# Attention logits by joined products, alternating heads, and a router constant made on VectorE, in a two-layer decoder trunk

## The chip, the cores and the metric

The kernel runs on one core of a Trainium2 chip. A core has five engines with queues of their own: TensorE (PE in the rows; its weight loads are PEld) multiplies matrices into PSUM, VectorE (DVE) and ScalarE (ACT) work element by element, GpSimd (POOL) is a slower third one for that, and SyncE (SP) here issues the loads from HBM. The metric is the time of one execution on the device in microseconds, the median of several.

## What is computed

Two layers over 256 tokens of width 1024. Each has a mixer and then 16 experts of which every token takes two. The parts that the change touches:

```
# layer 0, attention: 8 heads of width 64, blocks of 128 queries
z = einsum('bhqd,bhkd->bhqk', q[:, :, start:end], k[:, :, :end])
strict = s_pos < t_pos
log_keep = where(strict, log_sigmoid(-z), 0.0)
later = cumsum(log_keep, axis=3, reverse=True) - log_keep
a = where(strict, exp(log_sigmoid(z) + later), 0.0)
out = einsum('bhqk,bhkd->bhqd', a, v[:, :, :end])
# layer 1, gated linear attention: 4 heads of key width 64
scores = where(causal, einsum('nbhid,nbhjd->nbhij', q_in, k_in), 0.0)
# both layers, the experts' router
h = rmsnorm(x, norm_ffn[l]) * (1.0 + sc2) + sh2
scores = softmax(h @ router_w)
```

Since h is a scaled x plus a shift sh2 that is the same for all tokens, the router's logits are a product of x with scaled weights plus a constant, sh2 @ router_w, that holds for every token.

## The kernel before

The program is written out by hand: each engine runs its instructions in the order in which the code issues them, and waits on semaphores where an operand is not there or a buffer not free. Weights come through a ring of 16 buffers of 1 MB (`unit`, L67 and L69, and `weight`, L1224), loaded by SyncE in the order of their use as soon as a buffer is free. Jobs of the modulation vectors (`ada`, L188: products of 32 columns each) are put between other products by `fill`.

Layer 0 runs projections and convolution taps (`conv`: some taps on VectorE at L541, some on ScalarE at L555 and GpSimd at L556), then from about 106 to 151 us the attention in `even_mixer`. Its four steps cc take one pair of heads each; the keys and queries of the two heads lie on partitions 0 to 63 and 64 to 127 of `kT` and `qT`. `logits` (L602 to L606) makes z for both heads of a pair in two PSUM banks, one bank per head, 384 columns: 256 queries against the first 128 keys, 128 against the second 128, and a mask of large negative numbers that is added as a bf16 product of the identity with `maskb` to each diagonal block. `minus` (ScalarE L612, VectorE L614), `softplus` (ScalarE L618, L619) and `softplus2` (VectorE L622) turn z into what `sums` (TensorE L629 to L632) adds up; `weights` (VectorE L636, L637, ScalarE L638) gives the attention weights, `attend` (L649, L650) their products with the values, for head 0 on output partitions 0 to 63 and for head 1 on 64 to 127, and `attended` (ScalarE L654, VectorE L655) cuts the result in two parts. `logits` of pairs 0 and 1 stand ahead of the loop, those of 2 and 3 in its first two rounds.

After it come the group norm of the convolution (`group_norm`, L660 on) and the output products `po` (L451), whose weights ScalarE (L55) and VectorE or GpSimd (L56) cut into two parts first. Ahead of the second half of them, `Norm.weights` makes the gain gc (L365), the router's scaled weights rwg (L372, VectorE) and the router's constant rc (L375): 8 single-precision products on TensorE, whose left operand is one modulation column spread over 128 columns. Layer 1 does the same ahead of its own second half. ScalarE copies rc out of PSUM (L378); the route uses it after the logits.

A single-precision product appears in the trace as two passes (two weight loads and two MATMUL rows). In layer 1 `attention` is a generator of which every `yield` is followed by one step of a projection; its gated scores gs (L911) are two groups of four products, for heads with q = 0 (partitions 0 to 63) and q = 1 (64 to 127), each followed by the copies of the causal part (VectorE, L915). The products kv (L926) work on partitions 0 to 63 and 64 to 127 too, with outputs on either half of the partitions and in two banks.

Of the kernel before, what the change touches and what calls it, by code (L numbers as in the profile page):

```python
# [7 lines left out]
F32 = mybir.dt.float32  # L8
# [4 lines left out]
OP = mybir.AluOpType  # L13
AX = mybir.AxisListType
# [3 lines left out]
E = 16  # L18
# [11 lines left out]
def trunk(ctx: ExitStack, tc: tile.TileContext, x, c, ada_w, ada_b, norm_mix, norm_ffn,  # L30
# [5 lines left out]
    V, S, G, PE, SP = nc.vector, nc.scalar, nc.gpsimd, nc.tensor, nc.sync  # L36
# [3 lines left out]
    live = ctx.enter_context(tc.tile_pool(name="live", bufs=1))  # L40
# [3 lines left out]
    def bank(name):  # L44
        return psum.tile([128, 512], F32, tag="ps", name=name)
# [51 lines left out]
    ones = const.tile([128, 128], F32, name="ones")  # L97
# [29 lines left out]
    b = bank("vcol")  # L127
# [46 lines left out]
    arow = {}  # L174
# [78 lines left out]
    class Norm:  # L253
# [113 lines left out]
        def weights(self):  # L367

            l = self.l
            self.gain()  # L370
            self.w = live.tile([128, 8, E], F32, tag="rwg", name=f"rwg{l}")
            V.tensor_tensor(self.w, rw, self.g[:, :, None].to_broadcast([128, 8, E]), op=OP.mult)  # L372
            b = bank(f"rc{l}")
            for k in range(8):
                PE.matmul(b[:, 0:E], lhsT=mod[l][:, 3, k:k + 1].to_broadcast([128, 128]), rhs=rw[:, k, :],  # L375
                          start=k == 0, stop=k == 7)
            self.c = live.tile([128, E], F32, tag="rc", name=f"rc{l}")
            S.activation(self.c, b[:, 0:E], AF.Copy)  # L378

# [115 lines left out]
    def even_mixer(pool, n01, late):  # L495
# [100 lines left out]
        def logits(cc):  # L596

            z = zl[cc] = zz.tile([128, 2, 512], F32, tag="zz", name=f"z{cc}")
            for h2 in range(2):
                r = slice(64 * h2, 64 * h2 + 64)  # L600
                zh = z[:, h2]
                PE.matmul(zh[:, 0:128], lhsT=identb, rhs=maskb, start=True, stop=False)  # L602
                PE.matmul(zh[:, 0:128], lhsT=kT[r, cc, 0:128], rhs=qT[r, cc, 0:128], start=False, stop=False)
                PE.matmul(zh[:, 128:256], lhsT=kT[r, cc, 0:128], rhs=qT[r, cc, 128:256], start=False, stop=False)
                PE.matmul(zh[:, 256:384], lhsT=identb, rhs=maskb, start=False, stop=False)
                PE.matmul(zh[:, 256:384], lhsT=kT[r, cc, 128:256], rhs=qT[r, cc, 128:256], start=False, stop=True)  # L606


        def minus(cc):
# [33 lines left out]
        def attend(cc):  # L643
            ob = zl[cc] = bank(f"att{cc}")
            a = zs[cc]
            for h2 in range(2):
                hc = slice((2 * cc + h2) * 64, (2 * cc + h2) * 64 + 64)
                r = slice(64 * h2, 64 * h2 + 64)
                PE.matmul(ob[r, 0:256], lhsT=vn[:, 0, hc], rhs=a[:, h2, 0:256], start=True, stop=False)  # L649
                PE.matmul(ob[r, 128:256], lhsT=vn[:, 1, hc], rhs=a[:, h2, 256:384], start=False, stop=True)  # L650

        def attended(cc):
            hi, lo = (c[:, 4 + cc, :] for c in cats)
# [130 lines left out]
    def odd_mixer(pool, nrm, n11, late, project):  # L784
# [62 lines left out]
        def attention():  # L847
# [54 lines left out]
            V.tensor_copy(kdn, halves(b))  # L902
            yield

            for q in range(2):
                b = bank(f"gs{q}").rearrange("p (c i) -> p c i", c=4)
                o = slice(64 * q, 64 * q + 64)
                for t in range(2):
                    ts_ = slice(t * 128, t * 128 + 128)
                    for cc in range(2):  # L910
                        PE.matmul(b[:, 2 * t + cc, :], lhsT=kT[o, cc, ts_], rhs=qT[o, cc, ts_], start=True, stop=True)  # L911
                yield
                for t in range(2):
                    for cc in range(2):
                        V.copy_predicated(sc[:, t, 2 * cc + q], trii, b[:, 2 * t + cc, :])  # L915
            yield
            yield

            yield
# [732 lines left out]
```

## Time and profile before

| | us |
|---|---|
| median of 3 runs (795.85 to 861.59) | 797.86 |
| the profiled execution | 801.36 |
| its span, first to last instruction | 799.6 |
| TensorE busy | 736.6 (92%) |
| VectorE, ScalarE, GpSimd busy | 314.4, 235.1, 118.9 |
| loads: 280.59 MB read, mean | 352 GB/s |
| a convolution tap on VectorE (L541, 56 of them), mean | 0.736 |

Times in the rows count from the start of the span. A timeline row has the start, the length of the row from its first start to its last end, engine, line, operation, output and inputs, shapes and count; in brackets the idle time of the engine before it and what ended it. Layer 0's mixer lasts until about 200 us, its experts until about 415, layer 1's mixer until about 560, its experts until the end.

### The profile page before, as it was taken

Reading aid. Unit: us, or ns where it says so; the run is one execution under the profiler, and the core shown is the slowest. Engines: PE = TensorE matmul, PEld = TensorE weight load, DVE = VectorE, ACT = ScalarE, POOL = GpSimd, SP = SyncE. Lnnn points to the kernel's source line nnn. Section 1 sums busy time; section 2 is a strip of 40 time slices with the busy share of each in tenths; the row PEclk is TensorE's granted clock in tenths of the full one; section 3 lists DMA queues with packets and bytes.
Section 4 is the critical chain, followed back from the end, with each engine's and each line's share of the span. In section 5 each row is a group of like instructions: output and inputs, shape, how many; then the busy total and the mean of one; then the engine's idle time right before and its main releaser. Section 6 shows DMA issues by size and latency. Waiting matters only on the chain. (4 is left out here: it accounts for less than half of the span.)

```text
span 799.6 us, 10666 instructions
## 1 busy us (share of the span) xinstructions
PE 736.6 (92%) x4177; PEld 404.3 (51%) x4177; DVE 314.4 (39%) x563; ACT 235.1 (29%) x441; POOL 118.9 (15%) x168
## 2 busy tenths in 40 slices
PE   7898798998999999999697999999699999999985
PEld 4498555586434344353233677578434334434323
DVE  4459968575213112130115655453513123213114
ACT  3357647463102001110113543551402001001012
POOL 2347646222000000000014500010200000000000
PEclk9999989999999999999989999999899999999988
DMA  9999739954999999999999997495799999999991
GB/s 358 385 376 419 267 120 394 372 224 192 351 412 409 409 409 409 410 408 409 407 401 389 401 413 247 182 390 204 292 362 411 410 409 409 410 410 409 408 381 58
DMA packets 74718, 282.52 MB, mean 353 GB/s; under 512 B 5194, under 2 KB 6438, under 8 KB 69530
## 3 DMA queue, kind: packets, MB, share of 16 engines
q1 hardware_dynamic: 73122, 278.68, 89.0%
q0 software_dynamic: 1344, 2.64, 0.9%
q8 instruction: 37, 0.61, 0.3%
q10 hardware_dynamic: 184, 0.34, 0.1%
q14 instruction: 31, 0.25, 0.1%
HBM read 280.59 MB, written 1.05 MB: 352 GB/s over the span
## 5 line engine op out<-in xcount | busy, mean ns | idle before, releaser
L1240 PE MATMUL g<-w,xg 128*64 128x512 f32 x512 | 115.9, 601 | 1.9 <-DMA w<-in_moe_w_gate_dram 1.8
L1273 PE MATMUL dn<-w,at 128*64 128x512 f32 x448 | 105.6, 623 | 11.5 <-PEq L1372 5.7
L1240 PE MATMUL u<-w,xg 128*64 128x512 f32 x496 | 110.6, 594 | 1.9 <-DMA w<-in_moe_w_up_dram 1.9
L1273 PEld LDWEIGHTS dn<-w,at 128*64 128x64 f32 x448 | 32.3, 143 | 77.0 <-issue 59.9
L1252 DVE TENSOR_TENSOR act<-sg,u 128x512 f32<-128x512 f32 (+1 forms) x18 | 11.1, 628 | 152.6 <-PE u L1240 152.6
L1240 PEld LDWEIGHTS u<-w,xg 128*64 128x64 f32 x496 | 34.7, 137 | 71.6 <-issue 64.7
L1240 PEld LDWEIGHTS g<-w,xg 128*64 128x64 f32 x512 | 35.3, 138 | 69.4 <-issue 62.9
L421 PE MATMUL pj<-hT,g 128*128 128x256 f32 x480 | 62.5, 288 | 7.0 <-DVE g L56 4.6
L56 DVE TENSOR_TENSOR g<-wi,g 128x512 fp32r<-128x512 f32 x72 | 58.2, 816 | 25.6 <-ACT g L55 24.5
L421 PEld LDWEIGHTS pj<-hT,g 128*128 128x128 f32 x480 | 59.2, 193 | 10.7 <-DVE g L56 6.7
L416 PE MATMUL pj<-g,hT 128*128 128x512 f32 x192 | 51.2, 414 | 7.5 <-DVE g L56 3.6
L55 ACT ACTIVATE g<-wi 128x512 fp32r<-128x512 f32 x72 | 44.4, 626 | 39.7 <-PE pj L421 20.9
L451 PE MATMUL po<-cat,g 128*128 128x256 f32 x372 | 51.1, 290 | 2.5 <-ACT gsr L994 1.7
L188 PE MATMUL ada<-ad,cond 128*32 128x512 f32 x384 | 50.6, 632 | 0.0
L451 PEld LDWEIGHTS po<-cat,g 128*128 128x128 f32 x372 | 46.8, 196 | 6.7 <-ACT gsr L994 2.6
L416 PEld LDWEIGHTS pj<-g,hT 128*128 128x128 f32 x192 | 35.6, 194 | 22.3 <-DVE g L56 6.7
L556 POOL TENSOR_TENSOR yc<-yc,cv 128x256 f32<-128x256 f32 x45 | 38.7, 860 | 24.3 <-ACT cv L555 21.6
L541 DVE SCALAR_TENSOR_TENSOR yc<-yp,epar,yc 128x256 f32<-128x256 f32 x56 | 41.2, 736 | 1.0
L1305 ACT ACTIVATE ys<-y 128x512 fp32r<-128x512 f32 x28 | 16.9, 625 | 70.4 <-DVE y L1295 50.2
L1263 DVE COPY at<-at 128x512 f32<-128x512 f32 x14 | 9.7, 692 | 68.0 <-PE at L1262 68.0
L1299 ACT ACTIVATE y<-dn,cw 128x512 f32<-128x512 f32 x7 | 4.8, 687 | 107.4 <-PE dn L1273 107.4
L1248 ACT ACTIVATE sg<-g 128x512 f32<-128x512 f32 x14 | 8.4, 597 | 89.4 <-PE g L1240 86.3
(385 smaller groups left out, 886.4 us busy)
## 6 DMA issues: line engine op xcount, KB each, us to landing
w<-in_moe_w_gate_dram SPq DMA_DIRECT2D x64, 1024.0 KB, 16.1
w<-in_moe_w_up_dram SPq DMA_DIRECT2D x62, 1024.0 KB, 18.4
w<-in_moe_w_down_dram SPq DMA_DIRECT2D x61, 1024.0 KB, 18.2
ad<-in_ada_w_dram SPq DMA_DIRECT2D x48, 1024.0 KB, 8.9
wi<-in_w_in_even_dram SPq DMA_DIRECT2D x20, 512.0 KB, 13.0
wi<-in_w_in_odd_dram SPq DMA_DIRECT2D x14, 512.0 KB, 12.6
wo<-in_w_out_even_dram SPq DMA_DIRECT2D x4, 1024.0 KB
wo<-in_w_out_odd_dram SPq DMA_DIRECT2D x4, 1024.0 KB, 16.6
```

The lines of the kernel that those rows point to most:

```text
L55: S.activation(g[0], w, AF.Copy)
L56: (eng or V).tensor_tensor(g[1], w, g[0].bitcast(F32), op=OP.subtract)
L188: PE.matmul(acc[32 * j:32 * j + 32, :], lhsT=cond[:, k, :], rhs=w[:, k - (i if n == 2 else 2 * i), c0:c0 + 512], start=i == 0, stop=i == 4 ...
L416: PE.matmul(bs[t], lhsT=self.h[j][:, k, t * 128:(t + 1) * 128], rhs=g[i], start=k == 0 and p == 0, stop=k == 7 and p == 2)
L421: PE.matmul(bs[c // 2][:, (c % 2) * T:(c % 2 + 1) * T], lhsT=g[i][:, c * 128:(c + 1) * 128], rhs=self.h[j][:, k, :], start=k == 0 and c % ...
L451: PE.matmul(self.acc[kd // 2][:, (kd % 2) * T:(kd % 2 + 1) * T], lhsT=block(g[wi], kd % 4), rhs=cats[ci][:, k, :], start=start and kd % 2 ...
L541: V.scalar_tensor_tensor(yc[:, k], yp[:, k, j:j + T], epar[:, k, j:j + 1], yc[:, k], op0=OP.mult, op1=OP.add)
L556: G.tensor_tensor(y, y, p, op=OP.add)
L1240: PE.matmul(b[64 * e:64 * e + 64, :], lhsT=xg[:, k, o + 64 * e:o + 64 * e + 64], rhs=we[:, e, k % 2 * 512:k % 2 * 512 + 512], start=k == 0 ...
L1252: V.tensor_tensor(a[:, n], sg[:, n], ub[:, n], op=OP.mult)
L1273: PE.matmul(bs[h][64 * e:64 * e + 64, :], lhsT=at[k][:, 64 * e:64 * e + 64], rhs=r[:, e], start=k == 0, stop=k == 3)
L1305: S.activation(ys[:, 0, n], y[h], AF.Copy)
```

## The change

Four edits. In `logits` the two blocks of queries against the first 128 keys become one product of 256 columns, products of the two heads alternate, and one mask product per head over both diagonal blocks comes last. In `attend` the loops are exchanged. In layer 1 the products of the gated scores alternate between q = 0 and q = 1 in one group, and the copies follow in the two steps behind it. In `Norm.weights` the constant is summed over the 8 column blocks by a multiplication and a sum on VectorE (by_k, of_p), and one product with a matrix of ones adds over the partitions.

```diff
@@ Norm.weights
+            by_k = live.tile([128, E, 8], F32, tag="arow", name=f"rk{l}")
+            V.tensor_tensor(by_k.rearrange("p e k -> p k e"), rw, mod[l][:, 3, :, None].to_broadcast([128, 8, E]), op=OP.mult)
+            of_p = live.tile([128, E], F32, tag="ap", name=f"rp{l}")
+            V.tensor_reduce(of_p, by_k, axis=AX.X, op=OP.add)
             b = bank(f"rc{l}")
-            for k in range(8):
-                PE.matmul(b[:, 0:E], lhsT=mod[l][:, 3, k:k + 1].to_broadcast([128, 128]), rhs=rw[:, k, :],
-                          start=k == 0, stop=k == 7)
+            PE.matmul(b[:, 0:E], lhsT=ones, rhs=of_p, start=True, stop=True)
@@ logits
+            heads = [slice(64 * h2, 64 * h2 + 64) for h2 in range(2)]
+            for h2, r in enumerate(heads):
+                PE.matmul(z[:, h2, 0:256], lhsT=kT[r, cc, 0:128], rhs=qT[r, cc, :], start=True, stop=False)
+            for h2, r in enumerate(heads):
+                PE.matmul(z[:, h2, 256:384], lhsT=kT[r, cc, 128:256], rhs=qT[r, cc, 128:256], start=False, stop=False)
             for h2 in range(2):
-                r = slice(64 * h2, 64 * h2 + 64)
-                zh = z[:, h2]
-                PE.matmul(zh[:, 0:128], lhsT=identb, rhs=maskb, start=True, stop=False)
-                PE.matmul(zh[:, 0:128], lhsT=kT[r, cc, 0:128], rhs=qT[r, cc, 0:128], start=False, stop=False)
-                PE.matmul(zh[:, 128:256], lhsT=kT[r, cc, 0:128], rhs=qT[r, cc, 128:256], start=False, stop=False)
-                PE.matmul(zh[:, 256:384], lhsT=identb, rhs=maskb, start=False, stop=False)
-                PE.matmul(zh[:, 256:384], lhsT=kT[r, cc, 128:256], rhs=qT[r, cc, 128:256], start=False, stop=True)
+                PE.matmul(z[:, h2].rearrange("p (a t) -> p a t", a=2)[:, :, 0:128], lhsT=identb,
+                          rhs=maskb[:, None, :].to_broadcast([128, 2, 128]), start=False, stop=True)
@@ attend
-            for h2 in range(2):
-                hc = slice((2 * cc + h2) * 64, (2 * cc + h2) * 64 + 64)
-                r = slice(64 * h2, 64 * h2 + 64)
-                PE.matmul(ob[r, 0:256], lhsT=vn[:, 0, hc], rhs=a[:, h2, 0:256], start=True, stop=False)
-                PE.matmul(ob[r, 128:256], lhsT=vn[:, 1, hc], rhs=a[:, h2, 256:384], start=False, stop=True)
+            for t in range(2):
+                for h2 in range(2):
+                    hc = slice((2 * cc + h2) * 64, (2 * cc + h2) * 64 + 64)
+                    r = slice(64 * h2, 64 * h2 + 64)
+                    PE.matmul(ob[r, 128 * t:256], lhsT=vn[:, t, hc], rhs=a[:, h2, 256 * t:256 + 128 * t],
+                              start=t == 0, stop=t == 1)
@@ attention (layer 1)
-            for q in range(2):
-                b = bank(f"gs{q}").rearrange("p (c i) -> p c i", c=4)
-                o = slice(64 * q, 64 * q + 64)
-                for t in range(2):
-                    ts_ = slice(t * 128, t * 128 + 128)
-                    for cc in range(2):
+            bs = [bank(f"gs{q}").rearrange("p (c i) -> p c i", c=4) for q in range(2)]
+            for t in range(2):
+                ts_ = slice(t * 128, t * 128 + 128)
+                for cc in range(2):
+                    for q, b in enumerate(bs):
+                        o = slice(64 * q, 64 * q + 64)
                         PE.matmul(b[:, 2 * t + cc, :], lhsT=kT[o, cc, ts_], rhs=qT[o, cc, ts_], start=True, stop=True)
-                yield
+            yield
+            for q, b in enumerate(bs):
                 for t in range(2):
                     for cc in range(2):
                         V.copy_predicated(sc[:, t, 2 * cc + q], trii, b[:, 2 * t + cc, :])
-            yield
+                yield
             yield
```

In TensorE's queue the logits of pair 0 stood as follows: z_1078 is their PSUM tile, and both heads carry the same names, first head 0 from a mask to the next but one, then head 1.

```order
L602 LDWEIGHTS identb
L602 MATMUL z_1078<-maskb,identb 128x128
L603 MATMUL z_1078<-qT,kT 128x128
L604 MATMUL z_1078<-qT,kT 128x128
L605 LDWEIGHTS identb
L605 MATMUL z_1078<-maskb,identb 128x128
L606 MATMUL z_1078<-qT,kT 128x128
L602 LDWEIGHTS identb
L602 MATMUL z_1078<-maskb,identb 128x128
L603 MATMUL z_1078<-qT,kT 128x128
```

Now, at the same place, a row with x2 holds the product of head 0 and then that of head 1:

```order
L604 MATMUL z_1078<-qT,kT 128x256 x2
L606 MATMUL z_1078<-qT,kT 128x128 x2
L608 LDWEIGHTS identb
L608 MATMUL z_1078<-maskb,identb 128x2x128
L608 LDWEIGHTS identb
L608 MATMUL z_1078<-maskb,identb 128x2x128
```

Ten products have become six, and the masks have moved behind the products of both heads.

On VectorE, in layer 0 at the end of the weight cuts (g are cut weights, gc the gain, rwg the router's scaled weights, xT the residual), there stood:

```order
L56 TENSOR_TENSOR g_1617<-wo_1551,g_1617 128x512
L56 TENSOR_TENSOR g_1623<-wo_1549,g_1623 128x512
L365 SCALAR_TENSOR_TENSOR gc_1633<-mod_148,vcol 128x8
L372 TENSOR_TENSOR rwg_1635<-rw,gc_1633 128x128
L479 SCALAR_TENSOR_TENSOR xT<-po_1452,mod_148,xT 128x256 x2
```

and now there stands (rk is by_k, rp is of_p):

```order
L56 TENSOR_TENSOR g_1601<-wo_1535,g_1601 128x512
L56 TENSOR_TENSOR g_1607<-wo_1533,g_1607 128x512
L365 SCALAR_TENSOR_TENSOR gc_1617<-mod_148,vcol 128x8
L372 TENSOR_TENSOR rwg_1619<-rw,gc_1617 128x128
L374 TENSOR_TENSOR rk_1621<-rw,mod_148 128x8x16
L376 TENSOR_REDUCE rp_1623<-rk_1621 128x16
L481 SCALAR_TENSOR_TENSOR xT<-po_1436,mod_148,xT 128x256 x2
```

Two instructions have come in behind the last cuts.

On TensorE the same place reads, before (acol is a modulation column, po the output products, cat the mixer's result in two parts):

```order
L451 MATMUL po_1455<-cat_1077,g_1534 128x256
L451 MATMUL po_1455<-cat_1076,g_1534 128x256
L197 MATMUL acol_1626<-ident,arow_1446 128x128 x4
L375 MATMUL rc_1637<-rw,mod_148 128x16 x8
L451 MATMUL po_1452<-cat_1076,g_1553 128x256
L451 MATMUL po_1452<-cat_1077,g_1553 128x256
```

and now:

```order
L453 MATMUL po_1439<-cat_1077,g_1518 128x256
L453 MATMUL po_1439<-cat_1076,g_1518 128x256
L197 MATMUL acol_1610<-ident,arow_1430 128x128 x4
L378 MATMUL rc_1625<-rp_1623,ones 128x16
L453 MATMUL po_1436<-cat_1076,g_1537 128x256
L453 MATMUL po_1436<-cat_1077,g_1537 128x256
```

The one product that is left reads rp of VectorE, and stands where the eight stood, ahead of the second half of the output products. Layer 1 has the same order on both engines.

## Rows read from the trace of the kernel before

**Rows 1.** The page, rate of the transfers, 40 equal slices of the span.

```profile
GB/s 358 385 376 419 267 120 394 372 224 192 351 412 409 409 409 409 410 408 409 407 401 389 401 413 247 182 390 204 292 362 411 410 409 409 410 410 409 408 381 58
```

**Rows 2.** Busy time by window: PE, PEld, DVE, ACT, POOL, clock, DMA, GB/s.

```profile
185.00:188.00 3.00, 3.00 (x29) 3.00 (x27) 0.88 (x2) 0.05 (x1) 0.00 (x0) 1.00 0.02 8
...
218.00:221.00 3.00, 3.00 (x18) 1.00 (x16) 0.88 (x2) 0.00 (x0) 0.00 (x0) 1.00 1.03 419
```

**Rows 3.** Timeline of TensorE: start and end of logits (columns as told above).

```profile
105.78 0.22 PE L602 MATMUL z<-maskb,identb 128*128 128x128 bf16 x1 [0.69 <-ACT vn L589]
...
119.68 0.22 PE L602 MATMUL z<-maskb,identb 128*128 128x128 bf16 x1
...
122.42 1.06 PE L188 MATMUL ada<-ad,cond 128*32 128x512 f32 x8
```

**Rows 4.** Timeline of TensorE: values of the first pair, and what follows.

```profile
123.42 0.66 PE L649 MATMUL att<-zs,vn 128*64 128x256 f32 x4
...
123.90 0.40 PE L650 MATMUL att<-zs,vn 128*64 128x128 f32 x4
...
124.22 1.92 PE L188 MATMUL ada<-ad,cond 128*32 128x512 f32 x16
```

**Rows 5.** Timeline of TensorE in layer 1: gated scores, projection, kv.

```profile
486.23 1.16 PE L911 MATMUL gs<-gqT,gkT 64*128 64x128 f32 x8
487.32 1.66 PE L416 MATMUL pj<-g,hT 128*128 128x512 f32 x6
...
496.96 1.09 PE L926 MATMUL kv<-gvn,gkdn 64*64 64x128 f32 x24
```

**Rows 6.** Timeline of all engines: the attention's chain of the first pair, and 149.

```profile
105.62 1.93 ACT L555 ACTIVATE cv<-yp,epar 128x256 f32<-128x256 f32 x4
...
108.62 0.81 ACT L612 ACTIVATE zs<-z 128x768 f32<-128x768 f32 x1 [1.06 <-PE z L606]
...
112.30 0.96 DVE L622 SCALAR_TENSOR_TENSOR ze<-zs,ze 128x768 f32<-128x768 f32 x1 [0.96 <-ACT ze L619]
...
117.85 0.70 PE L629 MATMUL zc<-ze,later 128*128 128x256 f32 x2
...
119.88 0.69 DVE L636 TENSOR_TENSOR zs<-zs,zc 128x512 f32<-128x512 f32 x1 [3.19 <-PE zc L632]
...
149.06 1.10 PE L660 MATMUL gm<-yc,bones 128*128 128x512 f32 x2 [1.13 <-DVE yc L558]
```

**Rows 7.** Timeline around the router's constant in layer 0; last row from the route.

```profile
167.94 1.86 PE L375 MATMUL rc<-rw,mod 128*128 128x16 f32 x16
...
169.65 3.60 PE L451 MATMUL po<-cat,g 128*128 128x256 f32 x24
...
173.69 0.29 DVE L372 TENSOR_TENSOR rwg<-rw,gc 128x128 f32<-128x128 f32 x1
...
174.17 3.16 PE L451 MATMUL po<-cat,g 128*128 128x256 f32 x24
...
193.91 0.29 DVE L1053 TENSOR_REDUCE rank<-cmp 128x32 f32<-128x128 f32 x1
```

**Rows 8.** Timeline around the router's constant in layer 1.

```profile
536.54 1.96 PE L375 MATMUL rc<-rw,mod 128*128 128x16 f32 x16
...
538.35 0.61 PE L451 MATMUL po<-cat,g 128*128 128x256 f32 x3
...
540.17 0.29 DVE L372 TENSOR_TENSOR rwg<-rw,gc 128x128 f32<-128x128 f32 x1
```

**Rows 9.** Busy time by window, as rows 2: clock under logits, and after a wait.

```profile
110.00:112.00 2.00, 2.00 (x8) 1.52 (x7) 1.30 (x3) 1.51 (x2) 0.00 (x0) 0.50 0.03 8
...
564.00:568.00 4.00, 0.85 (x7) 0.76 (x8) 3.64 (x10) 1.86 (x3) 2.39 (x4) 0.77 1.03 418
568.00:572.00 4.00, 4.00 (x18) 3.23 (x18) 1.56 (x5) 1.13 (x2) 0.00 (x0) 0.50 0.79 320
572.00:576.00 4.00, 4.00 (x22) 1.79 (x20) 0.66 (x2) 0.56 (x1) 0.00 (x0) 0.88 0.25 69
```

## The prediction

> **What bounds the kernel now.** I read the page's time line first. The transfer rate [rows 1] stands at about 410 GB/s, and hardly moves, from the start of either expert stage on (slices 12 to 24 and 31 to 38); in the mixers before them it falls to between 120 and 300. A finer cut of the same view says why: 8 GB/s from 185 to 188 us, 419 from 218 [rows 2]. The ring of 16 weight buffers is full, and nothing loads until the experts' products free the first. So there are two regimes. In a mixer the path runs through TensorE and what it waits for; in an expert stage it runs through the transfers, whose amount is fixed and whose start hangs on the mixer's end. A microsecond won or lost in either mixer should therefore reach the end in full. All four edits lie in the mixers.
>
> Next the timeline by engine. The logits of one pair of heads take 2.74 us at full clock (119.68 to 122.42 [rows 3]); under the second pair, from 110 to 112, the granted clock is at half, 1.2 GHz [rows 9]. TensorE does not set the pace of attention alone: at 117.85 it reaches the first sums, whose operand had been ready since 112.30 + 0.96 = 113.26, but at 149.06 it waits for VectorE's convolution [rows 6]. In layer 0 the router's constant starts at 167.94 and the output products at 169.65; VectorE is at that time still cutting weights and makes the router's scaled weights only at 173.69 [rows 7]. Layer 1 has the same order: 536.54, 538.35 and 540.17 [rows 8].
>
> **The change, part by part.**
>
> *Logits.* Per pair of heads 12 single-precision passes of 128 columns and 4 mask products become 4 passes of 256 columns, 4 of 128 and 2 mask products of 256 columns. No row of before shows a product on rows 0 to 63 beside one on rows 64 to 127 over all columns. The nearest is kv: 24 passes of 128 columns in 1.09 us, 45 ns each, where gs, on one half of the rows, needs 1.16 us for 8 [rows 5]. kv splits rows and columns, and two column halves alone would take 12 x 0.136 = 1.6 us (0.136 is gs's 1.09 through 8), so its row halves ran together too. I take the heads as running side by side. Then the eight passes cost what the eight of the values cost, 0.80 us (123.42 to 124.22 [rows 4]); the masks at most 0.22 each [rows 3], of which I take 0.3 for both: 1.1 us, 1.6 less per pair. If the heads do not overlap, 4 x 0.24 (half of 123.42 to 123.90) + 4 x 0.136 + 0.3 = 1.8 us, 0.9 less.
>
> What of that reaches the end? The first pair starts at 105.78 [rows 3] and is done at 106.9 instead of 108.5. ScalarE's copy of it moves from 108.62 only to 107.55, because four convolution steps stand before it from 105.62 for 1.93 us [rows 6]; everything down to VectorE's last step moves by the same 1.07, so the operand of the sums is ready at 112.2. TensorE gets there in time: logits until 108.0, then 32 modulation passes, 3.6 us at full clock (16 take 1.92 [rows 4] with a tail). The sums start at 112.2, not 117.85. VectorE, which idled 3.19 us before 119.88 [rows 6], takes them up after its step for the second pair (0.96) and two taps (0.74 each by the page), from 112.2 on, so at 114.7; from there ScalarE and VectorE set the pace, and what the third and fourth pair save falls into TensorE's waits. Carried through the second pair (attention 6.7 earlier, ScalarE's next copy 6.3 earlier) the stretch to 149.06 moves up by **6.0 us**. Bounds: 6.4 if every ScalarE and VectorE row stays as it is; 4.8 if the heads run one after the other or the low clock of 108 to 116 stays.
>
> *Values alternated.* Nothing. The old order is products of head 0 twice, then of head 1 twice, yet the trace has all four passes of 256 columns from 123.42 and all four of 128 from 123.90 [rows 4]: the two column halves already run abreast. The Trainium skill (TensorE: Matmul & The Clock Gate, Part 3, The mechanism) says that products start strictly in program order; by it the old order would take 1.5 us per pair and the new 0.8. This trace, with 0.80 for the old, does not agree.
>
> *Gated scores alternated.* Two groups of 8 passes, 1.09 us each (486.23 to 487.32 [rows 5]), parted by a projection step, become one of 16 that alternate row halves. Side by side they take 1.09 and **1.1 us** go; one after the other only the second start, 0.2. TensorE has no wait near, so this counts.
>
> *Router's constant.* Removed: 8 products, 16 passes, 1.7 us to the next product, once per layer. Added: a multiplication and a sum on VectorE and one product. The price is not theirs but their place. In VectorE's queue they stand behind the last weight cut and the router's weights; in TensorE's queue the one product stands ahead of all of the output products, which before needed neither. Layer 0: the multiplication follows 173.69 by 0.25; it and the sum are like rows of 0.29 (128x128 at 173.69; 128 to 32 at 193.91 [rows 7]), started 0.3 apart; the sum ends near 174.55, the product starts at 174.6, two passes at 1.7/16 make 0.2, and the output products start at 174.8, 5.15 late. Before, their first 24 took 3.60, with waits for parts that are now there; later ones take 3.16 (174.17 [rows 7]): **+4.7 us**. VectorE's queue itself moves up with the logits, so this adds to their gain and isn't covered by it. Layer 1: 540.17 + 0.25 + 0.6 gives 541.1, output products at 541.3 against 538.35 [rows 8]: **+2.95 us**. Behind the waiting product stand all output products, the residual, the router and the experts' gather; nothing covers them, as rows 2 say. Bounds: 4.4 to 5.0 and 2.6 to 3.2, the added VectorE steps taking 0.15 to 0.45 each.
>
> *Clock.* TensorE now idles 6.6 us in layer 0 (167.94 to 174.6, all moved up) and 4.5 in layer 1. Where it idled before, in 560 to 567, the granted clock fell to the 1.2 GHz level for about 6.8 us (0.77, 0.50 and 0.88 of these 4-us windows, [rows 9]), of which the 1.8 in the first pass nearly idle (0.85 us busy in 4) and some 5.4 lie under work, which costs up to half, 2.7. In layer 0 more of the low stretch passes while it still waits. I take **+1.0** and **+1.5**, bounds 0 and 2.7 each.
>
> **Sum.** -6.0 + 4.7 + 1.0 = -0.3 in layer 0; -1.1 + 2.95 + 1.5 = +3.3 in layer 1; together **+3 us**. On the profiled execution, 799.6 of span and 801.36 in all, that is 802.6 and 804.4. The runs shown lie lower (median 797.86), so I forecast 797.9 + 3 = **801 us**. For faster and slower I use 2%, 16 us, about what a measurement of this kernel can tell from no change.
>
> **Rivals.**
>
> *The gains win.* The constant's wait turns out short, or its clock price nil, and 6.4 + 1.1 stand against little. For it: the constant needs only a modulation column and the router's matrix, both there long before, so any slack in VectorE's queue would serve. Against: its last cuts are fed by ScalarE in an order that the change leaves as it is. With half the waits (2.3 + 1.5) and no clock price: 797.9 - 7.5 + 3.8 = 794.2 us.
>
> *Heads don't overlap.* 4.8 and 0.2 against 4.7 + 2.95 and a clock price of 2.5 to 4: 797.9 + 6 = 804 us. The kv row speaks against it.
>
> *Values gain from the order.* If the two heads' values ran one after the other now (2 x 0.24 + 2 x 0.136 = 0.75 each), alternating would save 0.7, on the path only for the last pair: 800.3 us. Rows 4 speak against it. The strict order that the Trainium skill's page states is this case.
>
> *The transfers pace everything* and the mixers' shifts vanish: 797.9. The full ring [rows 2] speaks against it.
>
> *Slower, over 2%.* The clock, once down in the router's wait, stays down through the output products and logits behind it, 16 us or so (in layer 0 from 174.8 until shortly before the route's 193.91 [rows 7]), in both layers: each loses half of up to 16, so 797.9 + 0.5 + 16 = 814.4, and it decides from some 15.5 us of low clock per layer. Against: the longest low stretch that I read is 6.8.
>
> **How the numbers follow.** Forecast 0.65; heads not overlapping 0.14; gains win 0.12; values' order 0.03; transfers pace 0.04; clock stays down 0.02. The range takes the first three with their bounds: all good ends give -6.4 - 1.1 + 4.4 + 2.6 = -0.5, all bad ones -4.8 - 1.1 + 5.0 + 3.2 + 2.7 + 2.7 = +7.7; with 2 us between runs below, 795 to 806. Only the last rival comes near slower by 2%, none near faster: 0.01, 0.97, 0.02.
>
> **What would show it.** In the profile of the changed kernel: logits of a pair near 1.1 us (else 1.8); the first sums near 112; TensorE waiting for the constant's operand (rp) 6 us in layer 0 and 4 in layer 1; the values still 0.8; the scores one group of about 1.1. It is wrong if TensorE doesn't wait for rp, if the logits' chain lets the sums start later than 113, or if the experts' transfers don't move with the mixers.

## The result and the profile after

The changed kernel takes 802.52 us (median of 6 runs, 801.57 to 803.26) against 797.49 for the kernel before beside it: 1.0052 of it, 95% interval 1.0026 to 1.0077. The ratios here and below are estimated from the fast runs, with their intervals; they are not the quotients of the medians. The changed kernel is slower by some 5 us, inside the forecast range and inside 2%; the forecast was 801.

The profiled execution after took 801.57 us with a span of 799.8, that of before 801.36 with 799.6. The two spans hardly differ, although the medians do: the profiled execution of before lies almost 4 us above its median, and one reason for that is found below. So the traces are compared piece by piece, from one product to another within one execution. The names in the rows: z are the attention's logits, zc the sums, att the values, gm the group norm, gs the gated scores, pj projections, lg the router's logits, mb the route's mask and rk TensorE's products of it.

| us | before | after |
|---|---|---|
| TensorE busy | 736.6 | 727.4 |
| VectorE, ScalarE, GpSimd busy | 314.4, 235.1, 118.9 | 317.2, 234.9, 121.6 |
| output products po (372 passes), mean ns | 290 | 305 |
| from the first logits to the last gm | 43.28 | 36.90 |
| layer 0, from acol to the first lg | 10.80 | 18.10 |
| layer 1, from the first pj to kv | 57.99 | 56.70 |
| layer 1, from acol to the first lg | 11.98 | 17.55 |

The page's transfer rates are as in [rows 1]: about 410 GB/s in the expert stages, less in the mixers.

```profile
GB/s 359 384 376 420 265 245 368 342 203 126 357 410 410 410 409 410 409 409 409 407 399 388 400 413 277 185 394 178 262 378 411 409 410 409 408 409 409 408 392 61
```

TensorE's timeline after, in the order of the program: logits of the first two pairs and the first sums (against [rows 3, 6]), the values of the first pair [rows 4], the last group norm product, the gated scores, kv [rows 5].

```profile
105.71 0.70 PE L604 MATMUL z<-qT,kT 64*128 64x256 f32 x4 [0.69 <-ACT vn L591]
106.25 0.39 PE L606 MATMUL z<-qT,kT 64*128 64x128 f32 x4
106.57 0.39 PE L608 MATMUL z<-maskb,identb 128*128 128x256 bf16 x2
106.89 0.70 PE L604 MATMUL z<-qT,kT 64*128 64x256 f32 x4
...
112.34 0.70 PE L632 MATMUL zc<-ze,later 128*128 128x256 f32 x2 [0.64 <-DVE ze L625]
...
116.76 0.87 PE L653 MATMUL att<-zs,vn 128*64 128x256 f32 x8 [0.24 <-ACT zs L641]
117.56 1.92 PE L188 MATMUL ada<-ad,cond 128*32 128x512 f32 x16
...
142.61 1.10 PE L664 MATMUL gm<-yc,bones 128*128 128x512 f32 x2 [1.13 <-DVE yc L560]
...
486.58 1.16 PE L915 MATMUL gs<-gqT,gkT 64*128 64x128 f32 x16
487.67 4.43 PE L418 MATMUL pj<-g,hT 128*128 128x512 f32 x18
...
496.01 1.09 PE L931 MATMUL kv<-gvn,gkdn 64*64 64x128 f32 x24
```

A pair's logits take 1.18 us (105.71 to 106.89), the first sums start at 112.34, the values take 0.80 as before (116.76 to 117.56), the scores are one group of 1.09.

Around the router's constant of layer 0 the trace after has, on TensorE and VectorE (against [rows 7]):

```profile
160.99 0.65 PE L197 MATMUL acol<-ident,arow 128*128 128x128 f32 x4
168.25 0.58 PE L378 MATMUL rc<-rp,ones 128*128 128x16 f32 x2 [6.61 <-DVE rp L376]
168.67 5.40 PE L453 MATMUL po<-cat,g 128*128 128x256 f32 x24
174.00 1.06 PE L188 MATMUL ada<-ad,cond 128*32 128x512 f32 x8
...
179.09 1.06 PE L291 MATMUL lg<-rwg,xT 128*128 128x16 f32 x8
```

```profile
167.40 0.38 DVE L374 TENSOR_TENSOR rk<-rw,mod 128x128 f32<-128x128 f32 x1
167.82 0.29 DVE L376 TENSOR_REDUCE rp<-rk 128x16 f32<-128x128 f32 x1
```

And in layer 1 (against [rows 8]):

```profile
540.24 0.58 PE L378 MATMUL rc<-rp,ones 128*128 128x16 f32 x2 [4.58 <-DVE rp L376]
540.66 0.99 PE L453 MATMUL po<-cat,g 128*128 128x256 f32 x3
```

TensorE waits 6.61 and 4.58 us for rp; together it is the longest entry among its waits (11.2 us). During each wait the clock falls, and it is still down behind it. By windows of 2 us (columns as in [rows 2]; the third value from the end is the clock):

```profile
162.00:164.00 2.00, 0.00 (x0) 0.00 (x0) 1.99 (x2) 1.97 (x4) 1.38 (x1) 0.91 0.11 45
164.00:166.00 2.00, 0.00 (x0) 0.00 (x0) 1.97 (x4) 1.16 (x4) 1.35 (x2) 0.50 0.00 0
...
172.00:174.00 2.00, 2.00 (x11) 1.85 (x9) 0.00 (x0) 0.00 (x0) 0.00 (x0) 0.53 0.50 205
174.00:176.00 2.00, 2.00 (x17) 1.16 (x17) 0.88 (x2) 0.63 (x1) 0.00 (x0) 1.00 0.00 0
...
538.00:540.00 2.00, 0.00 (x0) 0.00 (x0) 1.93 (x4) 0.00 (x0) 1.13 (x1) 0.77 1.00 401
540.00:542.00 2.00, 1.76 (x8) 1.79 (x9) 0.10 (x1) 0.18 (x1) 0.00 (x0) 0.50 1.04 418
...
544.00:546.00 2.00, 2.00 (x11) 2.00 (x11) 0.00 (x0) 0.00 (x0) 0.00 (x0) 0.52 0.91 356
```

By these shares, with the windows left out between them at 0.50, the 1.2 GHz level held for 10.2 us in layer 0 (0.36 + 8 + 1.88) and 6.8 in layer 1. The first 24 passes of po took 5.40 us; 24 passes at full clock take 3.16 [rows 7].

### The profile page after: what moved, and what is told of

The parts are those of the page before. It is cut to its first block, busy times and chain, and to the rows that moved or that the text cites. A ratio compares the mean times of both kernels' runs of the same rounds, so it can differ in the third digit from the quotient of the medians.

```text
span 799.8 us, 10567 instructions
## 1 busy us (share of the span) xinstructions
PE 727.4 (91%) x4125; PEld 399.1 (50%) x4125; DVE 317.2 (40%) x567; ACT 234.9 (29%) x441; POOL 121.6 (15%) x168
## 5 line engine op out<-in xcount | busy, mean ns | idle before, releaser
L1278 PE MATMUL dn<-w,at 128*64 128x512 f32 x448 | 104.4, 617 | 11.2 <-PEq L1377 5.8
L453 PE MATMUL po<-cat,g 128*128 128x256 f32 x372 | 54.8, 305 | 2.5 <-ACT gsr L999 1.7
L453 PEld LDWEIGHTS po<-cat,g 128*128 128x128 f32 x372 | 50.8, 212 | 6.4 <-ACT gsr L999 2.6
```

The costliest lines, as they stand in the source:

```text
L453: PE.matmul(self.acc[kd // 2][:, (kd % 2) * T:(kd % 2 + 1) * T], lhsT=block(g[wi], kd % 4), rhs=cats[ci][:, k, :], start=start and kd % 2 ...
L1278: PE.matmul(bs[h][64 * e:64 * e + 64, :], lhsT=at[k][:, 64 * e:64 * e + 64], rhs=r[:, e], start=k == 0, stop=k == 3)
```

## The experiments

Theory: the joined logits and the alternating scores give what was forecast or a little more, the constant takes all of it back, by its wait and by the low clock behind it. Rivals: the wait alone, another wait in its place, a gain that the expert stages swallow, and, for the logits, which of the three edits (joining, alternation, masks last) gives the gain. That each head's two mask products became one belongs to the third; no run takes it back alone. The kernel before had medians of 799.27, 797.03 and 797.73 us (7, 33 and 14 runs) beside the three sets of experiments, so a difference of 1 us between two of these kernels is not resolved by times alone; there the traces are read.

**e1: the changed kernel with the old constant.**

```diff
...
-            V.tensor_reduce(of_p, by_k, axis=AX.X, op=OP.add)
             b = bank(f"rc{l}")
-            PE.matmul(b[:, 0:E], lhsT=ones, rhs=of_p, start=True, stop=True)
+            for k in range(8):
+                PE.matmul(b[:, 0:E], lhsT=mod[l][:, 3, k:k + 1].to_broadcast([128, 128]), rhs=rw[:, k, :],
+                          start=k == 0, stop=k == 7)
```

> The changed kernel with the router's constant as in the kernel before: 8 products on TensorE, no step on VectorE. Theory (the two traces read together: the constant's wait and the low clock behind it cost 7.3 us in layer 0 and 5.6 in layer 1, the logits give 6.5 and the gated scores 1.3, and all of that reaches the end): 6.5 + 1.3 = 7.8 us below the kernel before, 789.7 us at its median of 797.5. Rival A (my forecast's sizes: the constant costs 4.7 + 1.0 + 2.95 + 1.5 = 10.15, the gains are 7.1): 790.4, not to be told from the theory by this run. Rival B (the transfers pace the end and the mixers' shifts vanish in the expert stages): 797.5. Rival C (the 2.8 us that the trace of the changed kernel gives back in layer 1's route are real and belong to the constant; then of 5.0 us in all the gains can be only some 5.1): 792.4.

790.57 us, 0.9877 of before (0.9838 to 0.9916). The constant costs the changed kernel 802.52 - 790.57 = 12 us, and what the other edits gain does reach the end: rival B falls. In the trace TensorE goes from acol to lg in 10.81 us, as before, and the last gm stands 36.85 us behind the first logits.

**e2: the kernel before with the new constant alone** (the same lines the other way round).

> The kernel before with the router's constant of the changed one and nothing else. Theory: 7.3 + 5.6 = 12.9 us above the kernel before, 810.4. Rival A (the forecast's sizes, waits of 4.7 and 2.95 and a clock price of 1.0 and 1.5): +10.2, 807.6. Rival B (transfers pace the end): 0. Rival C (2.8 us given back in layer 1's route): +10.1. Rival D (the wait exists only because the logits brought TensorE to it early, the constant alone costs less): TensorE would wait under 4 us for the constant's operand in layer 0; theory says 6 to 6.7 there and 4.5 in layer 1.

809.61 us, 1.0118 of before (1.0077 to 1.0160): 10.3 more than beside it, 12.1 more than the 797.49 of the first comparison. TensorE's timeline has the wait of the changed kernel to 0.01 us, without any gain of the logits:

```profile
174.93 0.58 PE L378 MATMUL rc<-rp,ones 128*128 128x16 f32 x2 [6.62 <-DVE rp L376]
175.34 5.47 PE L453 MATMUL po<-cat,g 128*128 128x256 f32 x24
```

So rival D falls: the wait does not come from TensorE being early. The time alone does not part the theory's +12.9 from the forecast's +10.2. The trace does: from acol to lg it takes 18.16 us in layer 0 and 17.90 in layer 1, 7.4 and 5.9 more than before.

**e3: the kernel before with the new logits alone.**

> The kernel before with the joined, alternating logits alone. Theory: the stretch from the first logits to the last group norm product is 6.5 us shorter, all of it reaches the end: 791.0. Rival A (forecast: 6.0): 791.5. Rival B (the gain is lost again in waits for the weight cuts behind the attention, which ScalarE and VectorE make in their own time): 3 or less, 794.5 or more, with longer waits of the output products for their parts than the 0.54 and 0.22 us of before.

790.98 us, 0.9889 (0.9849 to 0.9928). The last gm stands 36.87 us behind the first logits (43.28 before): 6.41 gained, and po waits 0.55 and 0.21 us for its parts, as before. Rival B falls. This kernel has the old values, e1 the new: a pair takes 0.80 us in both (118.51 to 119.31 here), so alternating them does nothing.

**e4: VectorE's steps for the constant made early.**

```diff
...
+        n01.constant()
         parts = po.parts(1, 0, [(k, q) for q in range(2) for k in (2, 3, 0, 1)], buffers, (2, 4, 6))
...
```

`constant` makes by_k and of_p ahead of the cuts of the second half, in layer 1 too; it also writes them to other buffers.

> The changed kernel with VectorE's two steps for the constant moved ahead of the last weight cuts, where the modulation column has long been there; the one product on TensorE stays where it is. Theory (the place in VectorE's queue costs, not the steps or the product): TensorE's wait for the operand goes (11.2 us to under 0.3), the low clock behind it too, and the time falls below the one with the 8 products by the 1.7 - 0.2 us that the one product saves per layer, twice: 789.7 - 3.0 = 786.7. Rival A (another operand is late instead, the weights' second parts): as with 8 products, 789.7, with waits of the output products for their parts longer by 1.5 per layer. Rival B (the wait belongs to the product on TensorE, not to the queue of VectorE): the wait stays, about 802.

790.28 us, 0.9880 (0.9840 to 0.9919): the wait for rp is gone, 12 us with it, by a move in VectorE's queue. The further gain did not show in the time. In layer 1 it is there: acol to lg takes 10.42, 1.56 less than with eight products. In layer 0 rival A holds in part: the output products wait for another operand instead, but it is a part of cat and not, as the rival said, a part of the weights. There acol to lg takes 12.41 us in this trace, 1.6 more than with eight products: from 168.5 the granted clock is at 1.2 GHz for 3.4 us. e6 below has the same wait without such a stretch, and takes 10.80.

```profile
163.86 1.47 PE L456 MATMUL po<-cat,g 128*128 128x256 f32 x9
166.70 2.83 PE L456 MATMUL po<-cat,g 128*128 128x256 f32 x15 [1.37 <-DVE cat L746]
```

**e5: the waits filled.**

```diff
+            warm = bank(f"warm{l}")
+            for i in range((28, 18)[l]):
+                PE.matmul(warm, lhsT=onesb, rhs=onesb[:, None, :].to_broadcast([128, 4, 128]), start=True, stop=True)
             b = bank(f"rc{l}")
```

> The changed kernel with bf16 products of 512 columns, whose results nobody reads, on TensorE ahead of the constant's product: 28 in layer 0 and 18 in layer 1, about as long as the waits of 6.61 and 4.58 us. They separate the wait from the low clock behind it. Theory (the idle time brings the low clock, and it costs 5.40 - 3.16 = 2.2 us under the first 24 output products of layer 0 and 5.57 - 3.26 = 2.3 in layer 1): the clock stays up there, the first 24 output products take about 3.2 us, and the time falls by 4.5, from 802.5 to 798.0. Rival A (the forecast's clock terms, 1.0 + 1.5): 800.0. Rival B (the low clock comes from what the output products do, not from the idle time): 802.5 or more, with the low stretches where they are.

799.44 us, 1.0024 (1.0004 to 1.0043), 3.1 less than the changed kernel, by products that do nothing. The first 24 passes of po are back at 3.14 us, at full clock:

```profile
164.15 0.65 PE L197 MATMUL acol<-ident,arow 128*128 128x128 f32 x4
164.64 6.21 PE L379 MATMUL warm<-onesb 128*128 128x512 bf16 x28
171.42 0.37 PE L381 MATMUL rc<-rp,ones 128*128 128x16 f32 x2 [0.58 <-DVE rp L376]
171.64 3.14 PE L456 MATMUL po<-cat,g 128*128 128x256 f32 x24
...
179.79 1.06 PE L291 MATMUL lg<-rwg,xT 128*128 128x16 f32 x8
```

From acol to lg it is 15.64 us in layer 0 and 15.05 in layer 1 (532.24 to 547.29). That divides the price of the constant: the wait costs 15.64 - 10.80 = 4.84 and 15.05 - 11.98 = 3.07, the low clock 18.10 - 15.64 = 2.46 and 17.55 - 15.05 = 2.50. Rival B falls. Of the 4.96 us of clock only 3.1 arrive in the median. This trace has another low stretch instead, ahead of all that differs between the two kernels (0.84, 0.50 and 0.81 of the windows from 144 to 150), and the last gm to acol takes 20.02 us, not 18.38. The traces of e4, e7 and e9 have the stretch too, those of e1, e3, e6, e8, e10 and e11 not. How many executions have it isn't known. In layer 1's route this execution loses as much again: lg to rk takes 19.67 us, not 18.04, with a low stretch of 6.8 us in it.

**e6: the steps where they are, the product behind three quarters of the second half.**

```diff
@@ Norm.weights
-            b = bank(f"rc{l}")
-            PE.matmul(b[:, 0:E], lhsT=ones, rhs=of_p, start=True, stop=True)
...
@@ Output.second
+                if kd == 5:
+                    norm.constant()
```

Here `constant` is the product and its copy.

> The changed kernel with VectorE's two steps where they are, behind the last weight cuts, but the one product on TensorE put behind three quarters of the second half's output products. Theory (the product's place in TensorE's queue and the steps' place in VectorE's are harmful only together): no wait for the operand, the output products of layer 0 start when the last cut cat part is there (some 0.1 us earlier than with the 8 products), layer 1 gains the 1.5 of the removed products: 790.6 - 1.6 = 789.0. Rival (VectorE's two steps delay its residual steps, and with them the route): 790.6 or more.

790.12 us, 0.9913 (0.9883 to 0.9943). No wait for rp is left: either move alone, on VectorE or on TensorE, takes back the whole price, as the theory says. Layer 0 takes 10.80 us from acol to lg, with the wait of 1.37 us for cat, layer 1 10.24. The 1.6 us that the theory expected below e1 are in the trace (11.98 - 10.24 = 1.74 in layer 1) and not resolved by the times.

**e7 and e8: the logits without alternation, and without joining.**

```diff
             for h2, r in enumerate(heads):
                 PE.matmul(z[:, h2, 0:256], lhsT=kT[r, cc, 0:128], rhs=qT[r, cc, :], start=True, stop=False)
-            for h2, r in enumerate(heads):
```

```diff
-            for h2, r in enumerate(heads):
-                PE.matmul(z[:, h2, 0:256], lhsT=kT[r, cc, 0:128], rhs=qT[r, cc, :], start=True, stop=False)
+            for i in range(2):
+                for h2, r in enumerate(heads):
+                    PE.matmul(z[:, h2, 128 * i:128 * i + 128], lhsT=kT[r, cc, 0:128],
+                              rhs=qT[r, cc, 128 * i:128 * i + 128], start=i == 0, stop=False)
```

> The changed kernel with the joined products of head 0 ahead of those of head 1, masks last: the order alone is taken back. Theory (TensorE runs products on different halves of the rows side by side over a few instructions, as it did for the values in the old order): a pair still takes about 1.2 us and the time is that of the changed kernel, 802.5. Rival (the alternation makes the gain): 1.8 us per pair, the first sums about 1 us later, and 1.2 us more, 803.7.

> The changed kernel with three products of 128 columns per head instead of one of 256 and one of 128, heads alternating, masks last: the joining alone is taken back. Theory (columns count, not products: kv ran 24 passes of 128 columns on alternating halves in 1.09 us): 12 passes in about 0.8 us, a pair in about 1.2, the time of the changed kernel, 802.5. Rival (a fixed cost per pass makes the gain): 12 passes as far apart as before's, 1.6 us, a pair in 2.0, and some 1.5 us more, 804.0.

803.47 us (1.0049 to 1.0097 of before) and 802.60 (1.0039 to 1.0090). A pair takes 1.19 us in e7, whose rows follow, and 1.20 in e8; both rivals fall, since the last gm stands 36.88 and 36.86 us behind the first logits. (The values, which the expectation of e7 names as a case of row halves, are split by output columns; its own rows are the first here that show row halves overtaking.)

```profile
107.51 0.71 PE L604 MATMUL z<-qT,kT 64*128 64x256 f32 x4 [0.69 <-ACT vn L591]
108.05 0.40 PE L605 MATMUL z<-qT,kT 64*128 64x128 f32 x4
...
108.70 0.71 PE L604 MATMUL z<-qT,kT 64*128 64x256 f32 x4
```

**e9 and e10: masks between the heads, and masks last as the only edit left.** e9 is e7 with each head's mask inside the loop of its products (below, against e7); e10 takes back joining and alternation both, and keeps one mask product per head, last.

```diff
                 PE.matmul(z[:, h2, 256:384], lhsT=kT[r, cc, 128:256], rhs=qT[r, cc, 128:256], start=False, stop=False)
-            for h2 in range(2):
```

> The changed kernel with the joined products, head by head, and each head's mask right behind its own products, ahead of the other head. Theory (the runs before show 1.19 us per pair without alternation and 1.20 without joining, so what parted the heads in the kernel before were the mask products, which use all rows and stood between and inside them): a head alone takes 2 x 0.24 + 2 x 0.136 + 0.16, some 0.9, a pair 1.8 instead of 1.18, the first sums come 0.6 later, and 0.6 to 1.2 us are lost at the end: 803.1 to 803.7. Rival (the place of the masks does not matter, the smaller number of instructions does): 1.2 us per pair, 802.5.

> The changed kernel with neither joining nor alternation in the logits: three products of 128 columns of head 0, three of head 1, then one mask product per head. Theory (only the masks' place matters): 1.2 us per pair, the time of the changed kernel, 802.5. Rival (either joining or alternation is needed): 12 passes one behind the other at 0.136 and the masks, 2.0 us per pair, 803.3 to 804.

803.80 us (1.0047 to 1.0095) and 802.65 (1.0033 to 1.0078). In e9 the heads stand apart, 1.07 us each, a pair 2.13:

```profile
107.00 0.70 PE L604 MATMUL z<-qT,kT 64*128 64x256 f32 x2 [0.69 <-ACT vn L591]
107.54 0.38 PE L605 MATMUL z<-qT,kT 64*128 64x128 f32 x2
107.85 0.28 PE L606 MATMUL z<-maskb,identb 128*128 128x256 bf16 x1
108.07 0.70 PE L604 MATMUL z<-qT,kT 64*128 64x256 f32 x2
...
111.25 3.64 PE L188 MATMUL ada<-ad,cond 128*32 128x512 f32 x32
114.82 0.70 PE L630 MATMUL zc<-ze,later 128*128 128x256 f32 x2
```

The first sums come 7.82 us behind the first logits, not 6.63, and the last gm 38.21, not 36.90: putting the masks between the heads costs 1.3 us of the 6.4. In e10 a pair takes 1.52 us, between the theory's 1.2 and the rival's 2.0. The 0.33 more per pair fall into the wait before the sums (6.63 again), and the last gm stands at 36.87: with the masks last, neither joining nor alternation is needed for the gain.

But e9 also shows that the overlap of the heads is the smaller part of it: with the heads apart 43.28 - 38.21 = 5.1 of the 6.4 us remain. At the first sums most of it is the clock. In the trace of before the granted clock is at 1.2 GHz from 108.8 to 115.6 us, under the second pair's logits and part of the 32 modulation passes behind them:

```profile
108.52 0.23 PE L602 MATMUL z<-maskb,identb 128*128 128x128 bf16 x1
...
113.03 4.88 PE L188 MATMUL ada<-ad,cond 128*32 128x512 f32 x32
```

The pair took 4.51 us instead of 2.74, the passes 4.82 (to 117.85 [rows 6]) instead of e9's 3.57. These 3.0 us and the shorter pairs (2.13 instead of 2.74, twice) are the 4.25 by which e9's first sums come closer to the first logits (7.82 instead of 12.07 us). The clock falls 3.0 us behind the first logits in both traces with the old logits (before and e2) and stays up there in the eleven others. So the stretch went with the logits; what in the old ones brought it, no run shows.

**e11: e6 with GpSimd's steps held back.** In the trace after, layer 1 gives back 2.8 us between the logits and the route's rk (18.04 us, 20.86 before). That was no part of the forecast. e3, which has the old constant, gives them back too (18.03), and e1, with the same old constant, does not (20.86). VectorE, GpSimd and TensorE in e1:

```profile
555.25 1.29 DVE L1088 TENSOR_SCALAR rank<-rank 128x32 f32<-128x32 f32 x1
...
553.95 3.77 POOL L1135 TENSOR_TENSOR hn1l<-hf,hn1h 128x512 fp32r<-128x512 f32 x3 [0.30 <-ACT hf L1134]
...
550.13 1.92 PE L188 MATMUL ada<-ad,cond 128*32 128x512 f32 x16
557.83 0.20 PE L1095 MATMUL rk<-mb,sub 128*128 128x16 bf16 x1 [4.31 <-DVE mb L1091]
```

and in e3:

```profile
556.59 0.17 DVE L1086 TENSOR_SCALAR rank<-rank 128x32 f32<-128x32 f32 x1
...
557.89 4.23 POOL L1133 TENSOR_TENSOR hn1l<-hf,hn1h 128x512 fp32r<-128x512 f32 x3 [1.94 <-ACT hf L1132]
...
552.74 3.24 PE L188 MATMUL ada<-ad,cond 128*32 128x512 f32 x16
557.29 0.17 PE L1093 MATMUL rk<-mb,sub 128*128 128x16 bf16 x1
```

Where the modulation's 16 passes run at full clock, GpSimd's steps fall beside VectorE's route steps, and one of them takes 1.29 us instead of 0.17. Where a low stretch slows the 16 passes, ScalarE's copy of their sums and GpSimd's steps behind it come later, and the route is undisturbed. e1's profiled execution took 792.98 us, its other three 790.05 to 790.85. The thirteen traces agree: only before and e1 run the 16 passes at full clock (1.92 us), and only there VectorE's route steps of over 1 us stand ahead of rk. So by these traces what was given back is no gain of the change but a meeting that the profiled execution of before happened to have. e11 moves the last three of GpSimd's four steps in layer 1, and ScalarE's copies for them, behind the route's mask in the code, and makes them wait for the mask:

```diff
...
+            if mb is not None:
+                G.tensor_copy(pool.tile([128, 1], F32, name=f"after{l}"), mb[:, 0, 0:1])
...
```

> The kernel with the constant's product behind the output products (790.1), and in layer 1 GpSimd's last three low parts of the normed tokens (hn1l) held back until VectorE has made the route's mask mb. Theory (what the trace of the changed kernel gives back in layer 1's route is a meeting of GpSimd's steps with VectorE's, which some executions have and others don't, and not a gain of the change): VectorE's route steps take 0.17 to 0.20 in every execution, TensorE waits 2.3 to 2.5 us in each layer for mb and never 4.3, slow steps of 1.2 and 1.7 us stand behind mb instead, off the path, and the executions lie closer together at the lower end: 789 with a spread under 5 us. Rival A (the meeting costs nothing at the end): 790.1 as without. Rival B (the held parts themselves become what the experts' gather waits for): over 791, with a longer wait of the gather for hn1l than 0.52 us.

789.81 us (786.94 to 792.08), 0.9903 of before (0.9881 to 0.9924), the lowest of all, but not apart from e6, and its runs spread over 5.1 us, not under 5 as expected. TensorE waits 2.5 us for mb in layer 0 and not at all in layer 1. A low stretch lay under the modulation's passes in this execution too (2.58 us for the 16), so the trace does not show what the holding back does at full clock: this run is inconclusive.

## Why the prediction was right, and where it was not

| us | forecast | by the traces |
|---|---|---|
| logits | -6.0 | -6.4 |
| values | 0 | 0 |
| gated scores | -1.1 | -1.3 |
| constant's wait, layer 0 | +4.7 | +4.8 |
| constant's wait, layer 1 | +2.95 | +3.1 |
| low clock, layer 0 | +1.0 | +2.5 |
| low clock, layer 1 | +1.5 | +2.5 |
| sum | +3 | +5.2 |

The medians say +5.0. All steps held but the last two.

*Logits.* The chain was carried through rightly: the operand of the sums bounds them, and TensorE is there first (a wait of 0.64 us for it). The pair measured 1.18 for a forecast of 1.1, and the gain is at the forecast's upper bound of 6.4, the one with every ScalarE and VectorE row unchanged. The low clock of 110 to 112 [rows 9] is gone, as the forecast's taken value needed. The prediction counted on that without a row that gives a reason, and had 4.8 for the case that it stays. So a part of the hit is luck: by e9's rows beside those of before, 3.0 of the 5.4 us by which the sums come earlier are the clock's. Its rival "heads don't overlap" fell. The prediction did not ask which edit brings the overlap. e7, e8, e10 and e9 answer: the masks out of the way, which is worth 1.3 us. Four of them per pair, each over all rows, stood between the products in the kernel before.

*Values.* Nothing, as read from [rows 4]; the rows of e3 beside e1 confirm it. The Trainium skill (TensorE: Matmul & The Clock Gate, Part 3, The mechanism) says that products start strictly in the order of the program. The rows of e7 do not agree: there the products of 256 columns of both heads (x4 at 107.51) all start before any of 128 columns (108.05), although head 0's 128 columns stand ahead of head 1's 256 in the queue.

*Scores.* 16 passes in 1.09 us, and kv 1.3 us nearer to the projections (56.70 us in e1, 57.98 in e3, which has the old scores).

*The constant's wait.* Its place, not its work: TensorE was free 6.6 us before rp was there, as foreseen, and e4 and e6 remove the price by moving either end. The forecast of 174.8 - 6.0 = 168.8 for po's start compares with 168.67, by two misses that cancel: the logits gave 0.4 more, and at the low clock the product took 0.42 us (168.25 to 168.67) instead of 0.2.

*The clock.* Here the sum failed, within its bounds of 0 and 2.7. For layer 0 the prediction argued that more of the low stretch passes while TensorE still waits, and took 1.0. It assumed the 6.8 us long stretch of [rows 9]. The stretch was 10.2 us long: it began while TensorE idled and ended 5.2 us after po's start, so half of 5 us was lost. The length is not all: in e7 and e9 the stretch was 6.8 us long but began later in the wait, and 17.72 - 15.64 = 2.08 and 17.11 - 15.64 = 1.47 were lost. For layer 1 the prediction reads 1.8 us nearly idle and 5.4 under work out of 6.8, which don't add up; 6.8 - 1.8 leaves 5.0, and half of that is the 2.5 that was paid. I took 1.5 for no reason that a row gives. With 2.5 twice the forecast would have been 803.4.

*Rivals.* "The gains win" fell with the waits of 6.61 and 4.58 us, "the transfers pace everything" with e1 and e2, and "the clock stays down" with two stretches of 10.2 and 6.8 us.

## What to carry to other kernels

Cheaper work that replaces products on the engine that bounds must be ready where its result is queued: eight products of 1.7 us without a late operand were worth 12 us more than one product with one. Price a wait on TensorE with the low clock behind it, at half the time for which rows of the same trace show the clock down under the work that follows. If products on different row halves should run side by side, look first for what stands between them over all rows.

## What was not expected of the hardware

By e7 and e10 TensorE's overtaking reaches only so far. In e7 two products of head 0 (4 passes) stand ahead of head 1's first, and both heads' four passes of 256 columns take 0.54 us, as in the changed kernel; in e10 three products (6 passes) stand ahead, and a pair takes 1.52 us instead of 1.19. Its rows show where the heads meet: six passes of L605, of which only four are head 0's, ahead of the first of L607, which is head 0's third product.

```profile
107.04 0.82 PE L605 MATMUL z<-qT,kT 64*128 64x128 f32 x6 [0.69 <-ACT vn L591]
107.59 0.27 PE L607 MATMUL z<-qT,kT 64*128 64x128 f32 x1
107.69 0.27 PE L605 MATMUL z<-qT,kT 64*128 64x128 f32 x1
```

The low stretches of the clock lie at different places in traces of the same code: e5's has one at 145 us, that of the changed kernel, which is the same up to there, has none. And a low clock can go with a shorter time: in layer 1's route the traces in which it slowed the 16 modulation passes have GpSimd's steps away from VectorE's, and lg to rk takes 18.0 us in e3, 20.86 in e1.
